# Modulation steps taken in pairs in one layer's merges, moved out of the other's, and put between the seven products; the last down tiles split once

## The chip, the cores and the metric

The kernel runs on one core of a Trainium2 chip. The metric is the device time of one execution in microseconds (us), lower is better. Five engines work side by side, each through its own instructions in a fixed order: TensorE (PE; its weight loads are a row of their own, PEld), VectorE (DVE), ScalarE (ACT), GpSimd (POOL) and SyncE (SP), which here only issues transfers. An instruction whose input or buffer isn't ready holds up everything behind it on its engine.

## The reference

A two-layer generator over 512 latent tokens of width 1024 (with 256 context tokens beside them in layer 0). All is float32.

```python
for l in range(DEPTH):                       # DEPTH = 2
    need_ctx = l < DEPTH - 1
    sh1, sc1, g1, sh2, sc2, g2 = jnp.split(sc @ w_ada[l] + b_ada[l], 6, axis=-1)   # sc = silu(c)
    csh1, ... = jnp.split(scc @ w_ada[l] + b_ada[l], 6, axis=-1)                   # scc = silu(c_ctx)
    h = rmsnorm(x, norm1_g[l]) * (1.0 + sc1) + sh1
    hc = rmsnorm(ctx, norm1_g[l]) * (1.0 + csc1) + csh1
    y, yc = hybrid_mixer(h, hc, w_in[l], ..., need_ctx)
    x = x + g1 * y
    h = rmsnorm(x, norm2_g[l]) * (1.0 + sc2) + sh2
    x = x + g2 * swiglu(h, w_gate, w_up, w_down)
    # with need_ctx the same for ctx
return rmsnorm(x, final_norm_g)

def merge(a, b, c, gate, w_br, w_o):         # the end of hybrid_mixer
    g = jax.nn.sigmoid(gate)                 # gate: the last 3 x 1024 columns of h @ w_in
    m = g[0] * (a @ w_br[0]) + g[1] * (b @ w_br[1]) + g[2] * (c @ w_br[2])
    return m @ w_o
```

`hybrid_mixer` runs windowed attention, a bidirectional gated recurrence and a chunked gating MLP on `h @ w_in`. `w_ada[l]` is 1024 x 6144: six vectors of 1024 (shift, scale and gate for each half of a layer), the "modulation".

## The kernel before, in words

**Dense products.** Activations lie transposed, 128 channels by tokens, and every float32 value is split in two parts (high and low, a rounded float32r and the rest). `dense` multiplies one column tile of 128 weights with all tokens: per 128 rows of the weight three matmuls (high x high, high x low, low x high). Its weights come by `load_w`: one transfer into a raw buffer `wr` (line L283), the high half `wh` written by ACT (L295), the low half `wl` by DVE (L296). The ring of raw buffers has three places, those of `wh` and `wl` two each. `dense` takes weights from the list `early` instead, if something lies there.

**Modulation steps.** The product with `w_ada` isn't done on PE (except for the first four units). A *unit* is 512 of the 6144 columns of one layer, a *step* is 128 of the 1024 rows of one unit: a tile `wra` of 256 KB is loaded, and `ada_accum` adds it, times one scalar per partition, to an accumulator `acc` (the first of a unit's eight steps on ACT, L529, the others on DVE, L531). Layer 0's units and the first four of layer 1 have two accumulators (token and context conditioning), the later ones of layer 1 one. After the eighth step `ada_fold` transposes and sums the accumulator (L506, L507), and after a group of units `ada_spread` sends the sums through eight matmuls or four pairs (L516) into `mod`. The steps wait in a list, `ada_queue`. `fill` does one of them: its tile is loaded one step ahead into the only buffer of the pool `adaw` (L547), so each load is issued after the step before it. `fill_unit` does eight steps by four transfers of 512 KB, two steps each, into the ring `wr` that the weights use too (L629).

**Where they stand.** Layer 0 calls `fill_unit` after the recurrence heads 1 to 3 (24 steps). In the *merges* (three branches of eight column tiles `m`: a gate product `pg`, a branch product `pb`, a tanh on ACT, a multiply on DVE at L1320 or L1323, an add on POOL) `fill` stands twice per tile: in layer 0 in all three branches (48 steps), in layer 1 in the last two (32 steps, units 8 to 11). The feed-forward of layer 0 does 24 + 32 steps: one after each down tile of pieces of four, one after each call of `seven`, the rest in the last down product, which drains the list.

**Feed-forward.** The hidden width is cut in pieces, (4, 2, 4, 4, 4, 4) tiles in layer 0 and (5, 5, 6, 6) in layer 1. From the second piece on, layer 0 makes gate and up by `seven`, a seven-product scheme for two column tiles: three raw loads, four sums on POOL (L435, tiles `s`), four splits by ACT and DVE (L760, L761) and seven products on PE (L413). The last piece's down product runs token block by token block (512 and 256 tokens in layer 0, 256 and 256 in layer 1), so that the next norm can start on the first block while the second is multiplied; each block loads and splits the eight down tiles anew. `add_res` (L808) adds the result to the stream `X`; `start_settle` starts the norm's parts as a chain that is worked off between the products (sums of squares L678 and L680, `nt` L721, high L726 and L730, low L727 on POOL and L731 on DVE). Then `prefetch` loads and splits the first two weight tiles of the next layer.

**What sets the order.** The builder writes the program in one stream; a planner then orders each engine's instructions and transfers by what it expects to be ready, the earlier written first, so a modulation step can run ahead of where it was written. Larger tiles live in 27 `Pages` in on-chip memory, each of two halves, handed out by the builder's own clock.

Of the kernel before, what the change touches and what calls it, by code (L numbers as in the profile page):

```python
# [10 lines left out]
F32R = mybir.dt.float32r  # L11
# [5 lines left out]
P = 128  # L17
D = 1024
KD = 8
# [87 lines left out]
class Builder:  # L107
# [178 lines left out]
    def stationary(self, kt):  # L286
        return [pool.tile([P, KD, P], F32R, tag=tag, name=self.nm(tag))[:, 0:kt, :]
                for pool, tag in ((self.wh, "wh"), (self.wl, "wl"))]

    def load_w(self, wap, kt):  # L290
        nc = self.nc
        raw = self.load_raw(wap, kt)
        hi, lo = self.stationary(kt)
        r, h, o = (t.rearrange("p k c -> p (k c)") for t in (raw, hi, lo))
        nc.scalar.activation(out=h, in_=r, func=AF.Copy)  # L295
        nc.vector.tensor_tensor(out=o, in0=r, in1=h.bitcast(F32), op=ALU.subtract)  # L296
        return hi, lo
# [120 lines left out]
    def seven(self, w1, w2, q, take):  # L418

        nc = self.nc
        n = KD // 2 * P
        r1, r2 = (self.load_raw(w, KD).rearrange("p k c -> p (k c)") for w in (w1, w2))
        r3 = self.load_raw(w2[KD // 2 * P:, :], KD // 2).rearrange("p k c -> p (k c)")
        sa, sb = self.pair("s21"), self.pair("s34")  # L430
        s21, s34 = (t.ap.rearrange("p a b -> p (a b)")[:, 0:2 * n] for t in (sa, sb))
        s2, s1, s3, s4 = s21[:, 0:n], s21[:, n:2 * n], s34[:, 0:n], s34[:, n:2 * n]
        for o, x, y in ((s1, r2[:, 0:n], r2[:, n:2 * n]), (s2, s1, r1[:, 0:n]), (s3, r1[:, 0:n], r2[:, 0:n]),
                        (s4, s2, r1[:, n:2 * n])):
            nc.gpsimd.tensor_tensor(out=o, in0=x, in1=y, op=ALU.add)  # L435
        al = self.pd.tile([P, 1024], F32, tag="pd", name=self.nm("pa"))[:, 0:H]
        be, ga = self.bank("pb")[:, 0:H], self.bank("pg")[:, 0:H]
        tmp = self.single("ptmp")
        u1, u2, u5 = tmp[:, 0:H], tmp[:, H:T], tmp[:, 0:H]
        g1 = self.high_low(r1)  # L440
        self.product(al, g1, 0, q["B11"], True)
        nc.scalar.copy(out=u1, in_=al)
        self.product(be, g1, KD // 2, q["B21"], True)
        take(0, 0, be, u1)
        g2 = self.high_low(s21)
        self.free(sa)
        self.product(al, g2, 0, q["N2"], False)
        nc.scalar.copy(out=u2, in_=al)
        self.product(ga, g2, KD // 2, q["N1"], True)
        nc.scalar.copy(out=u5, in_=ga)  # L450
        g3 = self.high_low(s34)
        self.free(sb)
        self.product(al, g3, 0, q["T3"], False)
        take(1, 1, al, u5)
        self.product(ga, g3, KD // 2, q["B22"], False)
        take(0, 1, ga, u2)
        g4 = self.high_low(r3)
        self.product(al, g4, 0, q["T4"], False)
        take(1, 0, al, None)
        self.free(tmp)  # L460
# [160 lines left out]
            if self.ada_queue:  # L621
                self.ada_load()

    def fill_unit(self):

        assert self.ada_raw is None
        for _ in range(KD // 2):
            raw = self.wr.tile([P, 2, 512], F32, tag="wr", name=self.nm("wra"))
            self.nc.sync.dma_start(out=raw, in_=self.ada_rows_of(2))  # L629
            for j in (0, 1):  # L630
                self.ada_step(raw[:, j, :])
# [623 lines left out]
    def layer(self, l):  # L1255
# [14 lines left out]
        for hd in range(4):  # L1270
            if hd % 2 == 0:
                o.append(self.pair("op"))
            self.hgrn_head(l, hd, act, wcol, o[hd // 2][:, hd % 2, :], need_ctx)
            if hd == 0:
                self.x_out(tt)
            if l == 0 and hd > 0:
                self.fill_unit()
        self.attn_keys(act, wcol)
        at = []
        gm = self.gmlp(l, act, wcol, tt)  # L1280
# [18 lines left out]

        macc = []  # L1300
        if l == 1:
            self.ada_units(1, (8, 9, 10, 11), 1)
        for bi, (idx, src) in enumerate(((2, cc), (0, at), (1, o))):
            if bi == 2:
                self.x_back(tt)
            if bi == 1:
                self.finish_chains()
            br, brheld = self.split_pairs(src, tt, "br")
            for m in range(KD):
                pg = self.dense(wcol(OFF_GT + idx * D + m * P), act, [(0, tt)])  # L1310
                if l == 0 or bi > 0:
                    self.fill()
                gt = self.single("gt")
                nc.scalar.activation(out=gt[:, 0:tt], in_=pg[:, 0:tt], func=AF.Tanh, scale=0.5)
                pb = self.dense(a["w_branch"][l, idx][:, m * P:(m + 1) * P], br, [(0, tt)])
                if bi == 0:
                    if m % 2 == 0:
                        macc.append(self.pair("macc"))
                    mm = macc[m // 2][:, m % 2, 0:tt]
                    nc.vector.scalar_tensor_tensor(out=mm, in0=gt[:, 0:tt], scalar=1.0,  # L1320
                                                   in1=pb[:, 0:tt], op0=ALU.add, op1=ALU.mult)
                else:
                    nc.vector.scalar_tensor_tensor(out=gt[:, 0:tt], in0=gt[:, 0:tt], scalar=1.0,  # L1323
                                                   in1=pb[:, 0:tt], op0=ALU.add, op1=ALU.mult)
                    mm = macc[m // 2][:, m % 2, 0:tt]
                    nc.gpsimd.tensor_tensor(out=mm, in0=mm, in1=gt[:, 0:tt], op=ALU.add)
                self.free(gt)
                if l == 0 or bi > 0:
                    self.fill()
            self.free(*brheld)  # L1330
        self.free(*hheld)
        if l == 0:
            assert len(self.ada_queue) == 3 * KD
            self.ada_units(1, (4, 5, 6, 7), 1)
        else:
            assert not self.ada_queue
        self.dump(f"m{l}", macc[0][:, 0, :])
        mact, mheld = self.split_pairs(macc, tt, "m")
        g1 = self.small("g1", 16).rearrange("p (b k) -> p b k", b=2)
# [21 lines left out]
        for pi, n in enumerate(pieces):  # L1361
            last = pi == len(pieces) - 1
            gu, guheld = [], []
            for i in range(min(n, max(0, plain - f0))):
# [11 lines left out]
                self.split(s[:, 0:tt], hp[:, i % 2, 0:tt], lp[:, i % 2, 0:tt])  # L1376
                self.free(s)
                gu.append((hp[:, i % 2, :], lp[:, i % 2, :]))
                if l == 0 and i > 0:
                    next(making)  # L1380
                    if i > 1:
                        next(making)
# [8 lines left out]
            if last and l == 0:  # L1391
                self.norm_begin(1, ("n1g", 1, 2), 0, 1, "h")
            after = self.norm_shared if l == 0 else self.final_part
            for bi, blk in enumerate(blocks if last else [(None, 0, tt)]):
                for m in range(KD):
                    ps = self.dense(a["w_ffn_down"][l][f0 * P:(f0 + n) * P, m * P:(m + 1) * P], gu, [blk[1:]])
                    for bb in ([blk] if last else blocks):
                        self.add_res(m, ps, lambda b, m: self.mod[l][:, 40 + m, b:b + 1], bb)
                    if n > 2:
                        self.fill()  # L1400
                if last and bi == 0:
                    self.drain()
                self.finish_chains()
                if last and (l == 0 or bi == 0):
                    self.start_settle(blk, after, 0.0 if bi else PACE[1], l == 0)
# [127 lines left out]
```

## Time and profile before

| | |
|---|---|
| Median of 3 runs | 2484.31 us (2484.3 to 2485.63) |
| Profiled execution, its time | 2482.72 us |
| Its span, first to last instruction | 2480.9 us |
| PE busy | 2397.0 us (97%) |
| DVE, ACT, POOL busy | 1555.1, 900.3, 308.9 us |
| Mean granted PE clock | 0.993 |
| Read and written in HBM | 230.45 and 7.34 MB, 96 GB/s over the span |

In the profile, idle time of an engine before an instruction is put down to what released it. The time of a matmul's end is modelled, so a PE that waits a little between matmuls can still be shown as busy; the length of a stretch against the same work in an undisturbed stretch tells more. Tile names are those of the program without their numbers.

### The profile page before, as it was taken

The page shows a single profiled execution, that of the slowest core. Times are in us where ns is not written, and L with a number is a line of the kernel's source. Part 1 is how long each engine was busy: PE and PEld are TensorE (multiplying, and loading weights), DVE is VectorE, ACT ScalarE, POOL GpSimd, SP SyncE. Part 2 cuts the span into 40 slices and gives each one's busy share as a digit, 9 for nine tenths or more (in the row PEclk, how much of TensorE's full clock was granted, in tenths as well). Part 3 has the DMA queues.
Part 4 walks back from the last instruction along what each step waited for, and adds up shares of the span by engine and source line. Part 5 has one row for each costly group of instructions (what it writes and reads, how often), then busy time and mean ns, then how long its engine had stood idle before and what let it go on. Part 6 is the DMA issues. An engine that isn't in the chain of part 4 may idle for free. (4 is left out here: it accounts for less than half of the span.)

```text
span 2480.9 us, 34528 instructions
## 1 busy us (share of the span) xinstructions
PE 2397.0 (97%) x13606; PEld 2083.7 (84%) x13606; DVE 1555.1 (63%) x2644; ACT 900.3 (36%) x1508; POOL 308.9 (12%) x215
## 2 busy tenths in 40 slices
PE   8999999999999999999999989999999999999998
PEld 3888888888788888889999978888887779888888
DVE  4688777875544366767666676678885457434335
ACT  3333344442122243233433453335453235322224
POOL 0000100000111120222232331000000112000001
PEclk9999999999999999999999999999999999999999
DMA  8222111123442241333343341111215455233334
GB/s 295 70 77 81 48 43 35 39 64 112 142 133 73 78 118 43 115 111 110 95 127 111 107 144 52 43 43 52 60 44 152 124 151 168 79 106 100 91 103 130
DMA packets 370673, 240.02 MB, mean 97 GB/s; under 512 B 9744, under 2 KB 341968, under 8 KB 370512
## 3 DMA queue, kind: packets, MB, share of 16 engines
q1 hardware_dynamic: 366576, 225.24, 30.6%
q0 software_dynamic: 2304, 10.49, 1.2%
q8 instruction: 107, 1.75, 0.3%
q10 hardware_dynamic: 1632, 2.10, 0.2%
q14 instruction: 54, 0.44, 0.1%
HBM read 230.45 MB, written 7.34 MB: 96 GB/s over the span
## 5 line engine op out<-in xcount | busy, mean ns | idle before, releaser
L295 ACT ACTIVATE wh<-wr 128x1024 fp32r<-128x1024 f32 (+4 forms) x344 | 308.0, 895 | 853.1 <-PE pd L313 727.2
L313 PE MATMUL pd<-hh,wl 128*128 128x512 f32 (+1 forms) x1504 | 451.9, 356 | 21.5 <-DVE wl L296 21.4
L296 DVE TENSOR_TENSOR wl<-wr,wh 128x1024 fp32r<-128x1024 f32 (+4 forms) x344 | 354.9, 1032 | 186.8 <-ACT wh L295 184.1
L313 PE MATMUL pd<-hh,wh 128*128 128x512 f32 (+1 forms) x1504 | 459.9, 362 | 0.7 <-ACT wh L295 0.6
L313 PE MATMUL pd<-hl,wh 128*128 128x512 f32 (+1 forms) x1504 | 446.7, 354 | 0.0
L313 PEld LDWEIGHTS pd<-hh,wl 128*128 128x128 f32 x1504 | 249.0, 190 | 65.7 <-DVE wl L296 28.9
L531 DVE SCALAR_TENSOR_TENSOR acc<-wra,sc,acc 128x512 f32<-128x512 f32 x224 | 169.6, 778 | 186.7 <-DMA wra<-in_w_ada 175.6
L313 PEld LDWEIGHTS pd<-hl,wh 128*128 128x128 f32 x1504 | 248.2, 190 | 34.4
L313 PEld LDWEIGHTS pd<-hh,wh 128*128 128x128 f32 x1504 | 249.7, 191 | 31.4 <-ACT wh L295 1.0
L313 PE MATMUL pd<-fh,wl 128*128 128x512 f32 (+1 forms) x496 | 175.3, 370 | 0.3 <-DVE wl L296 0.3
L313 PE MATMUL pd<-fl,wh 128*128 128x512 f32 (+1 forms) x496 | 175.7, 370 | 0.0
L313 PE MATMUL pd<-fh,wh 128*128 128x512 f32 (+1 forms) x496 | 174.4, 369 | 0.6 <-ACT silu L1370 0.6
L313 PE MATMUL pd<-guh,wh 128*128 128x512 f32 (+1 forms) x576 | 172.6, 341 | 1.8 <-ACT guh L760 0.9
L313 PE MATMUL pd<-guh,wl 128*128 128x512 f32 (+1 forms) x576 | 172.5, 340 | 1.8 <-DVE wl L296 1.8
L313 PE MATMUL pd<-gul,wh 128*128 128x512 f32 (+1 forms) x576 | 172.9, 340 | 0.1
L808 DVE SCALAR_TENSOR_TENSOR X<-pd,mod,X 128x256 f32<-128x256 f32 (+1 forms) x160 | 84.1, 560 | 85.3 <-PE pd L313 84.9
L313 PEld LDWEIGHTS pd<-guh,wh 128*128 128x128 f32 x576 | 98.3, 188 | 15.4 <-ACT guh L760 1.2
L313 PEld LDWEIGHTS pd<-guh,wl 128*128 128x128 f32 x576 | 98.6, 189 | 15.1 <-DVE wl L296 2.6
L313 PEld LDWEIGHTS pd<-gul,wh 128*128 128x128 f32 x576 | 98.7, 189 | 13.4 <-DVE gul L761 0.9
L313 PEld LDWEIGHTS pd<-fh,wl 128*128 128x128 f32 x496 | 90.1, 188 | 17.4 <-DVE wl L296 1.2
L313 PEld LDWEIGHTS pd<-fh,wh 128*128 128x128 f32 x496 | 89.5, 188 | 16.8 <-ACT silu L1370 0.8
L313 PEld LDWEIGHTS pd<-fl,wh 128*128 128x128 f32 x496 | 90.0, 188 | 15.5
(285 smaller groups left out, 4432.9 us busy)
## 6 DMA issues: line engine op xcount, KB each, us to landing
wr<-in_w_in SPq DMA_DIRECT2D x116, 512.0 KB, 3.9
wra<-in_w_ada SPq DMA_DIRECT2D x136, 256.0 KB, 2.8
wr<-in_w_ffn_gate SPq DMA_DIRECT2D x44, 512.0 KB, 3.9
wr<-in_w_ffn_up SPq DMA_DIRECT2D x44, 512.0 KB, 3.9
wr<-in_w_out SPq DMA_DIRECT2D x32, 512.0 KB, 3.7
wr<-in_w_branch SPq DMA_DIRECT2D x48, 256.0 KB, 3.0
wr<-in_w_ffn_down SPq DMA_DIRECT2D x48, 256.0 KB, 2.8
wr<-in_w_ffn_down SPq DMA_DIRECT2D x24, 384.0 KB, 3.3
```

What stands on the lines that cost most here:

```text
L295: nc.scalar.activation(out=h, in_=r, func=AF.Copy)
L296: nc.vector.tensor_tensor(out=o, in0=r, in1=h.bitcast(F32), op=ALU.subtract)
L313: nc.tensor.matmul(ps[:, b0:b1], lhsT=w[:, k, :], rhs=x[:, b0:b1], start=b not in first, stop=(k == kt - 1 and i == 2), skip_group_check=True)
L531: nc.vector.scalar_tensor_tensor(out=acc[:, 0:512], in0=w, scalar=sc, in1=acc[:, 0:512], op0=ALU.mult, op1=ALU.add)
L808: self.nc.vector.scalar_tensor_tensor(out=self.X[m][:, c0:c1], in0=ps[:, c0:c1], scalar=gcol(b, m), in1=self.X[m][:, c0:c1], op0=ALU.mult, ...
```

## The change

Four edits. (1) In layer 0's merges, one `fill_pairs()` after each column tile (one transfer of 512 KB into `wr`, two steps) takes the place of two `fill` calls. (2) Layer 1's merges do no steps: units 8 and 9 of layer 1 join the list after layer 0's merges and are done in layer 0's feed-forward, units 10 and 11 in layer 1's first gate and up tiles, two pairs after each of the first four. (3) Each `seven` gets one more `fill`, after its second product; layer 1's down products have none. (4) In the last piece of either layer, `keep_w` splits each down tile once, from `wr` into a page, and both token blocks use it through `early`.

```diff
+    def keep_w(self, wap, kt):
+        pg = self.pair("wk", F32R)
+        hi, lo = pg[:, 0, 0:kt * P], pg[:, 1, 0:kt * P]
+        self.split(self.load_raw(wap, kt).rearrange("p k c -> p (k c)"), hi, lo)
+        return pg, tuple(t.rearrange("p (k c) -> p k c", c=P) for t in (hi, lo))
...
         take(0, 0, be, u1)
+        self.fill()
         g2 = self.high_low(s21)
...
-    def fill_unit(self):
-        assert self.ada_raw is None
-        for _ in range(KD // 2):
+    def fill_pairs(self, n=1):
+        for _ in range(n):
+            if not self.ada_queue:
+                return
+            assert self.ada_raw is None
             raw = self.wr.tile([P, 2, 512], F32, tag="wr", name=self.nm("wra"))
             self.nc.sync.dma_start(out=raw, in_=self.ada_rows_of(2))
             for j in (0, 1):
...
             if l == 0 and hd > 0:
-                self.fill_unit()
+                self.fill_pairs(4)
...
         if l == 1:
-            self.ada_units(1, (8, 9, 10, 11), 1)
+            self.ada_units(1, (10, 11), 1)
...
                 pg = self.dense(wcol(OFF_GT + idx * D + m * P), act, [(0, tt)])
-                if l == 0 or bi > 0:
-                    self.fill()
...
                 self.free(gt)
-                if l == 0 or bi > 0:
-                    self.fill()
+                if l == 0:
+                    self.fill_pairs()
...
             self.ada_units(1, (4, 5, 6, 7), 1)
-        else:
-            assert not self.ada_queue
+            self.ada_units(1, (8, 9), 1)
...
                 gu.append((hp[:, i % 2, :], lp[:, i % 2, :]))
-                if l == 0 and i > 0:
+                if l == 1:
+                    self.fill_pairs(2)
+                elif i > 0:
...
-                    ps = self.dense(a["w_ffn_down"][l][f0 * P:(f0 + n) * P, m * P:(m + 1) * P], gu, [blk[1:]])
+                    wap = a["w_ffn_down"][l][f0 * P:(f0 + n) * P, m * P:(m + 1) * P]
+                    if last:
+                        if bi == 0:
+                            kept.append(self.keep_w(wap, n))
+                        self.early.append(kept[m][1])
+                    ps = self.dense(wap, gu, [blk[1:]])
+                    if last and bi == 1:
+                        self.free(kept[m][0])
...
-                    if n > 2:
+                    if l == 0 and n > 2:
                         self.fill()
```

More of the change, by code (lines that the diff above doesn't have):

```diff
@@ L1393, in layer @@
             after = self.norm_shared if l == 0 else self.final_part
+            kept = []
             for bi, blk in enumerate(blocks if last else [(None, 0, tt)]):
                 for m in range(KD):
-                    ps = self.dense(a["w_ffn_down"][l][f0 * P:(f0 + n) * P, m * P:(m + 1) * P], gu, [blk[1:]])
+                    wap = a["w_ffn_down"][l][f0 * P:(f0 + n) * P, m * P:(m + 1) * P]
[6 more added lines that the diff above has]
+                        self.free(kept[m][0])
                     for bb in ([blk] if last else blocks):
                         self.add_res(m, ps, lambda b, m: self.mod[l][:, 40 + m, b:b + 1], bb)
-                    if n > 2:
+                    if l == 0 and n > 2:
                         self.fill()
@@ L1402, in layer @@
                     self.drain()
+                assert l == 0 or not self.ada_queue
                 self.finish_chains()
```

## The prediction

> **What bounds the kernel now.** First the page: which engine fills the span, and what the idle time of the others waits for.
>
> ```profile
> span 2480.9 us, 34528 instructions
> PE 2397.0 (97%) x13606; PEld 2083.7 (84%) x13606; DVE 1555.1 (63%) x2644; ACT 900.3 (36%) x1508; POOL 308.9 (12%) x215
> L531 DVE SCALAR_TENSOR_TENSOR acc<-wra,sc,acc 128x512 f32<-128x512 f32 x224 | 169.6, 778 | 186.7 <-DMA wra<-in_w_ada 175.6
> wra<-in_w_ada SPq DMA_DIRECT2D x136, 256.0 KB, 2.8
> wr<-in_w_in SPq DMA_DIRECT2D x116, 512.0 KB, 3.9
> ```
>
> PE is the bound, and none of the four edits takes a matmul of the model away. All there is to win is time in which PE stands still. The third row says where to look: DVE stood 175.6 us in front of modulation steps whose tile had not landed, with its other work queued behind them. Busy shares don't tell whether PE paid for that, so the second view is the stretches of the changed stages, with undisturbed ones beside them as a rate.
>
> ```profile
> core 0: us, PE busy (x) PEld busy (x) DVE busy (x) ACT busy (x) POOL busy (x), PEclk, DMA share, GB/s
> 552.15:846.89 294.74, 283.95 (x1602) 246.01 (x1601) 146.76 (x207) 70.49 (x92) 34.70 (x19) 0.99 0.37 110
> 754.48:791.92 37.44, 37.44 (x219) 33.01 (x218) 10.52 (x13) 8.03 (x11) 6.70 (x3) 1.00 0.29 85
> 577.85:578.65 0.80, 0.80 (x10) 0.80 (x9) 0.00 (x0) 0.48 (x1) 0.00 (x0) 1.00 0.56 196
> 1878.84:2053.97 175.13, 167.71 (x721) 135.35 (x720) 83.80 (x106) 52.12 (x75) 26.92 (x18) 0.99 0.50 146
> 1953.40:1994.20 40.80, 40.80 (x182) 33.78 (x181) 16.00 (x21) 13.81 (x21) 8.37 (x5) 1.00 0.38 110
> 1024.84:1424.12 399.28, 387.29 (x2195) 366.27 (x2194) 266.24 (x374) 143.01 (x219) 104.33 (x68) 1.00 0.37 108
> 1175.05:1204.17 29.12, 29.12 (x170) 28.94 (x169) 17.89 (x22) 12.48 (x19) 12.68 (x9) 1.00 0.32 92
> 1141.40:1174.68 33.28, 33.21 (x191) 28.81 (x191) 25.14 (x39) 6.97 (x10) 5.33 (x4) 1.00 0.48 144
> 1424.12:1476.85 52.73, 46.19 (x252) 38.86 (x251) 39.97 (x63) 28.46 (x48) 21.58 (x20) 0.97 0.56 164
> 2118.06:2162.02 43.96, 43.92 (x192) 36.07 (x193) 15.12 (x17) 12.38 (x17) 0.00 (x0) 1.00 0.31 90
> 2434.02:2473.50 39.48, 39.48 (x328) 38.84 (x327) 29.53 (x54) 23.06 (x48) 11.47 (x11) 1.00 0.47 143
> ```
>
> Layer 0's merges, 552.15 to 846.89: 1602 matmuls are 22 column tiles of 72 and two spreads of 8 (and two at the edges). Three tiles take 37.44 us undisturbed, 12.48 each, so 22 take 274.56, and the spreads 1.6 (0.80 each). 294.74 - 276.2 = 18.6 us lost. Layer 1's, 1878.84 to 2053.97: 20 tiles of 36 matmuls at 40.80 / 5 = 8.16 us are 163.2, so 11.9 us lost. The stretch of the seven products: 18 calls at 29.12 / 2 = 14.56 (262.1), three down products of four at 33.28 (99.8), one of two at half of that (16.6); 399.28 - 378.5 = 20.7, of which 0.8 is a spread: 19.9 lost. In layer 1's first gate and up tiles and its last down product PE is busy throughout: nothing to win there.
>
> Third, who stopped PE. The first three rows are layer 0's merges, the next two layer 1's, then DVE (658.21, 659.54) and PE at one such place.
>
> ```profile
> DVE acc L531 <- DMA wra<-in_w_ada: 73.1, 34, 6.9
> PEld pd L313 <- DVE wl L296: 13.3, 8, 3.5
> PE pd L313 <- DVE wl L296: 10.8, 8, 3.1
> DVE acc L531 <- DMA wra<-in_w_ada: 57.8, 25, 5.3
> PE pd L313 <- DVE wl L296: 7.3, 6, 3.0
> 658.21 1.42 DVE L531 SCALAR_TENSOR_TENSOR acc<-wra,sc,acc 128x512 f32<-128x512 f32 x2 [3.99 <-DMA wra<-in_w_ada]
> 659.54 1.22 DVE L296 TENSOR_TENSOR wl<-wr,wh 128x1024 fp32r<-128x1024 f32 x1
> 660.81 0.62 PE L313 MATMUL pd<-hh,wl 128*128 128x512 f32 x2 [1.27 <-DVE wl L296]
> ```
>
> DVE waits 3.99 us for a step's tile, then does it, then splits the next gate weight; PE has used up its high half and waits. The tile came late because its load goes out only when the one buffer is free.
>
> **The change part by part.** *Pairs in layer 0's merges.* 48 loads of 256 KB become 24 of 512 KB in the ring of three that the weights use; the steps' DVE and ACT work stays the same. The nearest rows are the heads of layer 0, which already take pairs through that ring (first two rows; heads, 12 pairs), against single loads in the merges (third row):
>
> ```profile
> L629 SPq DMA_DIRECT2D wra<-in_w_ada x12: 367/368/372, 95.5 to 238.2; - x12
> DVE acc L531 <- ACT acc L529: 5.8, 3, 2.2
> L547 SPq DMA_DIRECT2D wra<-in_w_ada x43: 327/328/340, 553.1 to 755.3; - x43
> ```
>
> There DVE waited 5.8 us for 12 pairs, 0.48 each (behind ACT's first step, which waited for the tile); here 73.1 for 43 single loads, 1.7 each. 24 pairs at 0.48 are 11.6 us of waiting, a sixth of 73.1, and a sixth of the 18.6 lost is 3. The ring is busier here than in the heads, so I leave 4.6: **-14**. Ends: -18.6 if all goes; +10 if the weights come late (first rival). On SP the pair stands between the branch load of one tile and the gate load of the next, which therefore waits until the pair before has been accumulated. A serial turn of 3.9 (landing), 4 x 0.78 (accumulations), 3.9 (gate landing) is 10.9 of the 12.48 us that a tile takes: covered, with 1.6 to spare.
>
> *No steps in layer 1's merges.* 32 loads and their accumulations leave; tiles without them run at 8.16 us in the undisturbed stretch. I leave 0.9 of the 11.9: **-11**, ends -11.9 and -8 (waits on POOL's or ACT's part that the steps now hide). The spread at their end moves with the steps.
>
> *16 more steps in layer 0's feed-forward, 18 of its calls to `fill` between products.* Same single buffer, same kind of wait:
>
> ```profile
> DVE acc L531 <- DMA wra<-in_w_ada: 35.6, 32, 2.4
> 1019.50 3.44 DVE L531 SCALAR_TENSOR_TENSOR acc<-wra,sc,acc 128x512 f32<-128x512 f32 x2 [1.20 <-DMA wra<-in_w_ada]
> 1031.74 0.45 PE L413 MATMUL pa<-np,wl 128*128 128x384 f32 x1 [2.07 <-DVE wl L761]
> L761 DVE TENSOR_TENSOR wl<-s,wh x36: 1205/1226/2322, 1030.1 to 1415.1; 128x1024 fp32r<-128x1024 f32 x36
> 1020.65 3.45 POOL L435 TENSOR_TENSOR s<-s,wr 128x512 f32<-128x512 f32 x2
> ```
>
> If every lost microsecond of the stretch were due to its 56 steps, one would cost 19.9 / 56 = 0.36, and 16 more 5.7; at best they fit in DVE's idle third and cost 0. I take **+3**, the middle, since some losses there, as that at 1031.74, come from DVE's backlog and others from POOL's sums, which no step touches. A third group means one more spread on PE: **+0.8**. What stands queued behind an added step: the split of `s` for the next product (1.21 to 2.32 us by its row), then PE; on SP the raw loads of the next call.
>
> The stretched durations in these rows bring in a rule. Two accumulations at 1019.50 took 3.44 us together, where one takes 0.78 on the page, while POOL added: 0.94 more for each. The Trainium skill, "SBUF — State Buffer", section "Who interferes with whom", says that a DVE instruction with two inputs in on-chip memory and a GpSimd instruction that reads it lock each other out, the second waiting for the whole of the first. By it every added step that meets a sum pays for it; the trace agrees in kind. What that would do is the third rival.
>
> *Eight pairs in layer 1's first gate and up tiles.* Four loads of 512 KB in the time of one gate and one up tile, 2 x 43.96 / 8 = 10.99 us, through three places. `w_out`'s loads, the densest there are, are issued thus:
>
> ```profile
> 2085.09 6.91 SPq L283 DMA_DIRECT2D wr<-in_w_out  x3
> ```
>
> Three in 6.91 with the last one's own 0.37, so one per 3.27. Four at that pace take 13.1, 2.1 over, 8.4 for four tiles: the upper end. Lower end 0: PE is never idle here now. Three 3.27 periods fit, so the fourth load slips only if the ring is also late; accumulations (16 x 0.78 = 12.5 us) fit in DVE's idle 28.8. **+2**.
>
> *Last down products split once.* In layer 0's (the stretch from 1424.12) the second block runs while DVE does the first block's norm. First two rows DVE, third ACT, from 1449 on; the last two are PE's waits over the stretch and the longest of them:
>
> ```profile
> L296 DVE TENSOR_TENSOR wl<-wr,wh 128x512 fp32r<-128x512 f32 x6 | 5.5, 913 | 1.1 <-ACT wh L295 1.1
> L296 DVE TENSOR_TENSOR wl<-wr,wh 128x1024 fp32r<-128x1024 f32 x2 | 3.5, 1748 | 0.0
> L295 ACT ACTIVATE wh<-wr 128x512 fp32r<-128x512 f32 x6 | 3.8, 629 | 3.2 <-DMA wr<-in_w_ffn_down 2.5 <-PE pd L313 0.6
> PE pd L313 <- DVE wl L296: 5.1, 4, 3.3
> 1470.89 0.50 PE L313 MATMUL pd<-hh,wl 128*128 128x512 f32 x1 [3.33 <-DVE wl L296]
> ```
>
> Eight splits at 0.913 go from a DVE that is the bound there (23.29 of 26 us busy, by the window row below), and eight loads from the queue ahead of `prefetch`, whose split ends the 3.33 us wait of layer 1's first product. PE waits 5.1 us in all for DVE's splits; the norm's own parts are late next, so I take **-4.5**, ends -5.1 and 0 (the norm takes its pages from what the eight kept ones leave). In layer 1's, PE is busy already: 0; its tail after the last product holds no weight work.
>
> ```profile
> 1449.00:1475.00 26.00, 19.46 (x122) 16.51 (x121) 23.29 (x37) 15.95 (x29) 11.53 (x10) 0.93 0.54 155
> ```
>
> Sum: -14 - 11 + 3 + 0.8 + 2 - 4.5 = -23.7 us. The profiled execution took 2482.7, so 2459.0; the median is 1.6 above it: **2460.6 us**.
>
> **The rivals.** *The pairs starve the weights (slower).* In layer 0's merges a load that takes 5 us instead of 3.9 makes the serial turn 5 + 3.1 + 5 = 13.1, over 12.48, and DVE's split behind it (1.22 in the row above) then lies open. The other edits win 9.7, so with the 18.6 lost now this decides from 28.3 / 24 = 1.2 us per tile on; at 2.0 it is 48 - 28.3 = 19.7 above before: 2504. Against it: the 512 KB loads land in 3.9 at the median. Chance 0.07.
>
> *The wait only changes its tile.* The pair's longer landing makes DVE wait half as often and twice as long, and PE loses what it lost: -2 for -14, so 2472.6. For it: the order on DVE is still fixed ahead, and 34 waits of DVE brought 8 of PE. Against: the heads' 0.48. Chance 0.16.
>
> *Added steps and POOL's sums lengthen each other.* If each of the 16 meets a sum and its 0.94 reaches PE, that is 15 instead of 3: 2472.6. For it: the sums feed the very next product. Against: POOL is busy 104.33 of the stretch's 399.28 us, so one step in four would meet one, and DVE is idle a third of the time. Chance 0.1. *Pages are short.* With eight kept, layer 1's norm waits for them and the 4.5 is not won: 2465.1; chance 0.05.
>
> *All waits go:* -18.6 - 11.9 - 5.1 + 0.8 = -34.8, 2449.5, chance 0.06. Several small ones cancel the gain to within 5 us: 0.06.
>
> **How the numbers follow.** My forecast has 0.5. About 0.2% (5 us) is what a measurement tells from no change. Faster: 0.5 + 0.16 + 0.1 + 0.05 + 0.06 = 0.87, less 0.03 for costs that no row shows, 0.84; same 0.07; slower 0.09, the first rival and a part of that. The range of 2446 to 2480 takes in every case but the first rival and the cancelling one; the likeliest alone spans 2452 to 2469.
>
> **What would show it.** Right: in layer 0's merges DVE's wait for `wra` falls from 73.1 to some 12 us and a tile takes close to 12.48; layer 1's merges run at 8.16 per tile; layer 1's first product waits less than 1 us; PE stays busy through layer 1's gate and up tiles. Wrong: ACT's `wh` waiting for raw weights in the merges; PE's waits for L761 in the seven products growing by more than 6 us; ACT's `wh` waiting for gate or up loads in layer 1.

## The result

The changed kernel takes 2470.39 us (median of 4 runs, 2468.26 to 2472.7), the kernel before 2484.31: a ratio of 0.9948, interval 0.993 to 0.9965, so 13.9 us less. Forecast were 23.7 us less. The sign and the range hold, and 10 us of the forecast gain are missing.

The page after the change: PE's idle time is smaller (77.5 us of the span, 83.9 before), and so is DVE's before the steps (151.7 us in front of L539 where L531 had 186.7). Lines stand 7 to 10 higher than before.

```profile
span 2470.9 us, 34332 instructions
PE 2393.4 (97%) x13614; PEld 2081.4 (84%) x13614; DVE 1535.7 (62%) x2628; ACT 889.6 (36%) x1492; POOL 309.1 (13%) x215
L539 DVE SCALAR_TENSOR_TENSOR acc<-wra,sc,acc 128x512 f32<-128x512 f32 x224 | 169.7, 783 | 151.7 <-DMA wra<-in_w_ada 124.0
```

The same stretches of work as in the prediction, from the view of windows (length, then busy time and count of PE, PEld, DVE, ACT and POOL, granted clock, DMA share, GB/s): layer 0's merges, layer 1's merges, the seven products, layer 0's last down product with layer 1's first products, layer 1's heads up to its merges, its first gate and up work, its second gate and up tiles, its last down product.

```profile
555.88:837.50 281.62, 281.62 (x1602) 244.38 (x1601) 144.02 (x205) 71.04 (x92) 35.09 (x19) 1.00 0.39 116
1875.29:2038.49 163.20, 163.20 (x721) 135.13 (x720) 57.01 (x70) 50.30 (x72) 26.10 (x17) 1.00 0.37 108
1013.97:1429.24 415.27, 392.33 (x2202) 366.90 (x2201) 281.07 (x401) 145.91 (x224) 106.92 (x68) 1.00 0.39 115
1429.24:1473.21 43.97, 43.12 (x249) 37.00 (x249) 28.33 (x47) 21.19 (x36) 20.76 (x19) 1.00 0.42 131
1466.64:1875.29 408.65, 398.80 (x2386) 341.88 (x2385) 305.91 (x612) 177.75 (x347) 35.34 (x25) 1.00 0.18 52
2088.64:2105.78 17.14, 14.34 (x104) 13.75 (x102) 12.67 (x27) 7.10 (x14) 1.15 (x1) 0.90 0.49 145
2105.78:2150.68 44.90, 44.85 (x200) 36.97 (x201) 24.18 (x32) 13.19 (x18) 0.00 (x0) 1.00 0.51 152
2422.68:2463.50 40.82, 39.28 (x328) 38.71 (x326) 18.48 (x42) 13.74 (x35) 8.12 (x11) 1.00 0.08 28
```

PE has no wait left in the merges, which are 13.1 and 11.9 us shorter. Layer 0's last down product and what follows fell from 52.73 to 43.97. The seven products, where the change adds steps, grew from 399.28 to 415.27: **16 us given back in one place**. The last two rows grew by 0.9 (the spread of units 10 and 11) and 1.3, and the row before them by 3.0 (14.1 us before for the same matmuls, at a granted clock of 1.00 where the row has 0.90).

Who stops PE there? First row: layer 0's merges; the others: the seven products.

```profile
DVE acc L539 <- DMA wra<-in_w_ada: 61.4, 16, 5.6
DVE acc L539 <- DMA wra<-in_w_ada: 51.4, 40, 3.2
PE pa L420 <- DVE silu L479: 9.7, 6, 3.1
PEld pa L420 <- DVE silu L479: 11.6, 6, 3.5
```

PE waits for L479, the combine that `take(1, 1)` hands to DVE. The fifth product lies in `pa` until that combine has read it, and the seventh needs `pa`. One such place, from the timeline (SP issues a step's load; DVE waits for it, accumulates, combines; PE goes on):

```profile
1082.30 0.46 SPq L555 DMA_DIRECT2D wra<-in_w_ada  x1
1085.56 1.41 DVE L539 SCALAR_TENSOR_TENSOR acc<-wra,sc,acc 128x512 f32<-128x512 f32 x2 [3.20 <-DMA wra<-in_w_ada]
1086.89 0.55 DVE L479 SCALAR_TENSOR_TENSOR silu<-pa,ptmp 128x384 f32<-128x384 f32 x1
1087.50 0.44 PE L420 MATMUL pa<-fh,wh 128*128 128x384 f32 x1 [2.66 <-DVE silu L479]
```

From this came **theory A**: the added steps cost PE 16 us because combines are queued on DVE behind steps that wait for a tile. Its rivals: the steps' work itself, not the waiting (D); and a step costs PE the same wherever it stands, so that taking it out here loses the same elsewhere.

### The profile page after: what moved, and what is told of

It reads as the page before. It is cut to its first block, busy times and chain, and to the rows that moved or that the text cites. A ratio compares the mean times of both kernels' runs of the same rounds, so it can differ in the third digit from the quotient of the medians.

```text
span 2470.9 us, 34332 instructions
## 1 busy us (share of the span) xinstructions
PE 2393.4 (97%) x13614; PEld 2081.4 (84%) x13614; DVE 1535.7 (62%) x2628; ACT 889.6 (36%) x1492; POOL 309.1 (13%) x215
## 5 line engine op out<-in xcount | busy, mean ns | idle before, releaser
L302 ACT ACTIVATE wh<-wr 128x1024 fp32r<-128x1024 f32 (+4 forms) x312 | 284.5, 912 | 802.2 <-PE pd L320 688.6
L303 DVE TENSOR_TENSOR wl<-wr,wh 128x1024 fp32r<-128x1024 f32 (+4 forms) x312 | 324.5, 1040 | 209.2 <-ACT wh L302 206.8
L539 DVE SCALAR_TENSOR_TENSOR acc<-wra,sc,acc 128x512 f32<-128x512 f32 x224 | 169.7, 783 | 151.7 <-DMA wra<-in_w_ada 124.0
L320 PE MATMUL pd<-guh,wh 128*128 128x512 f32 (+1 forms) x416 | 123.9, 354 | 1.4 <-ACT guh L770 0.9
L320 PE MATMUL pd<-gul,wh 128*128 128x512 f32 (+1 forms) x416 | 124.7, 356 | 0.4 <-DVE gul L771 0.2
L320 PE MATMUL pd<-guh,wl 128*128 128x512 f32 (+1 forms) x416 | 123.4, 353 | 0.0
L320 PEld LDWEIGHTS pd<-fh,wh 128*128 128x128 f32 x496 | 90.6, 190 | 17.1 <-ACT silu L1377 1.3
L690 POOL TENSOR_TENSOR sqa<-sqa,sq 128x256 f32<-128x256 f32 (+1 forms) x40 | 48.2, 1206 | 418.9 <-ACT sq L688 400.3
L1334 POOL TENSOR_TENSOR macc<-macc,gt 128x768 f32<-128x768 f32 (+1 forms) x32 | 62.2, 1943 | 269.0 <-DVE gt L1331 269.0
L320 PE MATMUL pd<-brl,wh 128*128 128x512 f32 (+1 forms) x288 | 87.7, 359 | 0.0
```

The costliest lines, as they stand in the source:

```text
L320: nc.tensor.matmul(ps[:, b0:b1], lhsT=w[:, k, :], rhs=x[:, b0:b1], start=b not in first, stop=(k == kt - 1 and i == 2), skip_group_check=True)
L539: nc.vector.scalar_tensor_tensor(out=acc[:, 0:512], in0=w, scalar=sc, in1=acc[:, 0:512], op0=ALU.mult, op1=ALU.add)
L690: eng.tensor_tensor(out=acc[:, c0:c1], in0=acc[:, c0:c1], in1=sq[:, c0:c1], op=ALU.add)
```

## The experiments

All kernels are edits of the changed one; of an edit the main lines are shown, `...` marks what is left out. Stretches run from the same matmul to the same matmul, so that they can be set side by side.

**No step between the products (e1_nomid).** Its 16 steps go to layer 0's merges, as a second pair per tile in the last branch.

```diff
         take(0, 0, be, u1)
-        self.fill()
...
-                    self.fill_pairs()
+                    self.fill_pairs(2 if bi == 2 else 1)
...
```

> The changed kernel without the step between the seven products; eight more pairs in the last branch of layer 0's merges do those 16 steps, so the feed-forward does 56 steps where it did them before. The stretch from the first to the last call of the seven products was 399.3 us before and 415.3 after. Theory A (the added steps make DVE wait for their tile, with the combining of two products, and so PE, queued behind): the stretch returns to 400 +- 3, and the merges stay at 12.5 to 12.8 us per tile with two pairs in each of eight tiles: about 2456 us. Rival B (the stretch is longer for another reason: kept pages, a slower rhythm of PE, the spreads): it stays at 411 or more, 2468 or more. Rival C (two pairs in one tile are too many for the ring of raw buffers): the stretch returns, but the last branch of the merges loses 8 us or more.

Measured: 2465.33 us (2462.24 to 2466.49), ratio 0.9922 [0.9905, 0.9939]. Layer 0's merges, `w_out` (the product that ends the mixer), the seven products:

```profile
555.23:843.34 288.11, 283.01 (x1603) 244.19 (x1602) 165.95 (x238) 73.05 (x96) 35.10 (x19) 1.00 0.44 127
843.34:921.31 77.97, 72.19 (x398) 62.57 (x397) 46.00 (x56) 31.44 (x42) 20.27 (x12) 0.96 0.37 107
1024.79:1422.50 397.71, 389.49 (x2203) 368.43 (x2202) 252.94 (x362) 143.87 (x220) 105.56 (x69) 0.99 0.37 110
```

The seven products are back at 397.7, so the added step alone makes the 16 us. But the merges (281.62 in the changed kernel) and `w_out` (73, at a clock of 1.00 where this row has 0.96) are 11.5 us longer: 2456 us as by theory A is missed, the merges lose 6.5 where rival C had 8 or more, and that place was no good.

**Tiles two ahead (e2_two).** The single loads go into halves of pages, two ahead.

```diff
-        self.ada_raw = self.aw.tile([P, 1, 512], F32, tag="aw", name=self.nm("wra"))
+        pg = self.single("wra")
+        raw = pg[:, 0:512].rearrange("p (k c) -> p k c", k=1)
...
-            if self.ada_queue:
+            while len(self.ada_raws) < min(2, len(self.ada_queue)):
                 self.ada_load()
...
```

> The changed kernel with the single loads of the modulation steps kept two ahead, in halves of pages, instead of one ahead in one buffer; the number of steps and their places are those of the changed kernel. Theory A (what costs is the wait for the tile, because the load goes out only after the step before): DVE's wait for these tiles in the stretch of the seven products falls from 51 us to 15 or less and the stretch from 415 to 400 or less, about 2456 us or less. Rival D (what costs is the work of the steps on DVE, and its contention with POOL's sums): the wait falls, but the stretch stays at 410 or more and the time within 4 us of 2470.

Measured: 2463.44 us (2461.04 to 2466.98), ratio 0.9917 [0.9899, 0.9936]. First the waits in the seven products, then the stretch in the view of windows:

```profile
PE pa L420 <- DVE silu L479: 12.6, 6, 2.9
DVE acc L539 <- DMA wra<-in_w_ada: 10.2, 8, 2.9
```

```profile
1010.88:1418.57 407.69, 389.87 (x2203) 368.62 (x2201) 279.86 (x390) 144.64 (x222) 101.04 (x68) 0.99 0.38 115
```

DVE's wait fell from 51.4 to 10.2, the stretch by 7.6 only, between what theory A (400 or less) and rival D (410 or more) expected, and PE stands before the combine as long as ever. Theory A alone is at best half of it.

**The last down tiles split twice again (e3_resplit).**

```diff
-                        if bi == 0:
-                            kept.append(self.keep_w(wap, n))
-                        self.early.append(kept[m][1])
...
```

> The changed kernel with the last down tiles loaded and split anew for each block, as before. If the splits taken from the second block are what shortened layer 0's last down product and the start of layer 1 (52.7 us before, 45.5 after): it returns to 51 to 54, and the wait of 1.5 us at the start of layer 1's last down product, which came with the kept tiles, goes: together 4 to 7 us slower than the changed kernel, 2474 to 2477. Rival (that stretch is shorter because no step is left in it, or because PE arrives later): it stays at 47 or less, and the time at 2470 or less.

Measured: 2475.02 us (2469.56 to 2477.32), ratio 0.9959 [0.9945, 0.9972]. The stretch of layer 0's last down product and what follows, and layer 1's last down product:

```profile
1421.67:1471.82 50.15, 45.66 (x251) 38.11 (x251) 37.29 (x60) 27.78 (x48) 21.53 (x20) 0.97 0.57 167
2420.68:2460.16 39.48, 39.48 (x328) 38.85 (x327) 29.52 (x54) 23.05 (x48) 11.47 (x11) 1.00 0.47 143
```

50.15 against 43.97: the edit is worth 6.2 us there, of which some 1.5 go with the lower granted clock of the row (0.97; the changed kernel has 1.00). In layer 1 it costs 1.3 (39.48 against 40.82): its splits run ahead on ACT and DVE, and the last tile of the hidden layer is split behind them. The one wait of PE in that stretch of the changed kernel:

```profile
PE pd L320 <- ACT guh L770: 1.5, 1, 1.5
```

**Layer 1's pairs in its merges (e4_l1merge).** Units 10 and 11 as one pair per tile of the second branch, none in the gate and up tiles.

```diff
-                if l == 0:
+                if l == 0 or bi == 1:
                     self.fill_pairs()
...
-                if l == 1:
-                    self.fill_pairs(2)
...
```

> The changed kernel with layer 1's eight pairs (units 10 and 11) one per tile in the second branch of layer 1's merges instead of in its first gate and up tiles. If the pairs run ahead into the norm of the second block and take DVE from it: the stretch from the end of layer 1's merges to its second gate tile, 67.3 us after and 64.1 before, returns to 64 or less, the merges stay at 8.16 us per tile (20 tiles 163.2), and the time falls by 3 to 5 us, 2466. Rival (a ring of three can't feed gate, branch and pair in 8.16 us): the eight tiles lose 1 us or more each, and the time stays or rises.

Measured: 2475.07 us (2474.31 to 2476.3), ratio 0.9962 [0.9949, 0.9975]. Layer 1's merges, its first gate and up work:

```profile
1872.07:2044.13 172.06, 167.56 (x730) 136.70 (x728) 71.42 (x90) 51.30 (x74) 25.39 (x17) 0.99 0.42 127
2093.49:2107.64 14.15, 12.96 (x104) 12.24 (x102) 9.36 (x22) 6.48 (x13) 0.71 (x1) 1.00 0.29 84
```

The first gate work falls from 17.14 to 14.15 and the second tile from 44.90 to 44.0, so the pairs cost 3.9 us where the change put them. In the merges they cost 8.9, 1.1 per tile (each figure holds their spread of 0.8): pairs are not free as such, and the rival's 1 us per tile came true. Layer 1's tile takes 8.16 us and holds less than layer 0's 12.5.

**No tile loaded, nothing to wait for (e5_noload).**

```diff
             self.ada_step(self.ada_raw[:, 0, :])
-            self.ada_raw = None
-            if self.ada_queue:
-                self.ada_load()
...
```

> Left out: all single loads of modulation tiles but the first; each such step adds the same loaded tile again, so the modulation of layer 1 is another. All accumulations stay where they are, and nothing waits for a tile. Theory A (the stretch of the seven products lost its 16 us to combines queued on DVE behind steps that wait for tiles): DVE's waits for modulation tiles vanish and the stretch falls from 415.3 to 400 us or less, near the 399.3 of the kernel before. Theory D (the steps' work on DVE itself, stretched where POOL adds, holds the combines up): the stretch stays at 406 or more, and PE goes on waiting for the first combine of the second half. Between the two both have a share.

**The same, with the step between the products in layer 1's heads (e10_noload_nomid).** The edit that takes the step out is that of e7_heads1 below.

> The single loads but the first are left out as in e5_noload (the modulation of layer 1 is another), and the step between the seven products is taken out, its 16 steps standing after layer 1's heads. With e5_noload (408.4 us for the stretch of the seven products) it gives the price of the 16 added steps where no step waits for a tile. If the waits of the steps that were there before cost PE something too, the stretch falls below e7_heads1's 399.9, to 390 or less; if only the added steps stand in PE's way, it stays at 396 to 401, and their price without waits is some 8 to 9 us.

**Both again, with POOL's sums replaced by copies on ACT (e11_noload_copies, e12_noload_nomid_copies).**

```diff
-            nc.gpsimd.tensor_tensor(out=o, in0=x, in1=y, op=ALU.add)
+            nc.scalar.copy(out=o, in_=x)
...
```

> As e5_noload, and the four sums of each call of the seven products, which POOL makes, are replaced by copies of their first operand on ACT (the products, and so the result, are others; the amount of work on PE and DVE is the same). Theory P (what the added steps cost beside waiting comes from POOL's sums: both last longer when they meet): accumulations take 0.75 to 0.80 us again instead of 1.0, and the difference of this run's stretch to that of e12_noload_nomid_copies is 3 us or less, where e5_noload and e10_noload_nomid differ by some 8. Rival Q (it comes from the place, on DVE's queue ahead of a combine for which PE waits): accumulations get shorter, but the difference stays at 6 us or more.

> As e11_noload_copies without the step between the seven products: its 16 steps stand after layer 1's heads. The stretch of this kernel is the base for e11_noload_copies: P expects the two within 3 us, Q this one at least 6 us shorter. Against e10_noload_nomid (sums on POOL, no step in the middle) it shows what POOL's sums cost the stretch by themselves: if the next product's split waits for the last sum, 3 us or more.

One profile of each (2467.59, 2450.95, 2443.39, 2436.74 us). The seven products in e5, e10, e11, e12, in this order:

```profile
1015.90:1424.27 408.37, 393.25 (x2200) 372.96 (x2201) 275.15 (x383) 144.57 (x222) 109.68 (x68) 0.98 0.26 77
```

```profile
1010.16:1403.56 393.40, 387.30 (x2192) 368.37 (x2193) 254.99 (x360) 143.58 (x219) 104.53 (x68) 0.99 0.27 79
```

```profile
1011.13:1401.09 389.96, 385.21 (x2203) 365.63 (x2201) 245.84 (x380) 181.28 (x290) 0.00 (x0) 1.00 0.28 80
```

```profile
1007.58:1392.34 384.76, 383.29 (x2195) 365.19 (x2194) 234.50 (x357) 180.44 (x288) 0.00 (x0) 1.00 0.28 81
```

| seven products, us | step between the products | step elsewhere | price of the 16 steps |
|---|---|---|---|
| tiles loaded, sums on POOL (changed kernel, e7) | 415.3 | 399.9 | 15.4 |
| no loads, sums on POOL (e5, e10) | 408.4 | 393.4 | 15.0 |
| no loads, no sums on POOL (e11, e12) | 390.0 | 384.8 | 5.2 |

**Theory A as the whole cause falls.** With nothing to wait for, e5's stretch is 408.4 where A wanted 400 or less, and the 16 steps still cost 15.0; e10's 393.4 lies between its two cases, and its 8 to 9 us as the price without waits is missed. Each price holds the third group's spread, 0.8. Two things in these rows keep the table from giving shares.

The first is the granted clock (the figure after POOL's in each row): PE had half of it for 17.1 us of e5's stretch, for 6.8 of e10's, for 3.4 of the changed kernel's and of e7's, and not at all in e11's and e12's. Two of e5's pieces:

```profile
1072.04:1075.45 3.41, 3.41 (x11) 3.41 (x12) 3.41 (x7) 2.37 (x4) 0.70 (x1) 0.50 0.51 147
1293.91:1300.73 6.82, 5.97 (x19) 5.97 (x20) 6.12 (x10) 2.00 (x3) 0.00 (x0) 0.50 0.44 129
```

At most half of these times was lost by it: 8.5, 3.4, 1.7 and 1.7 us. Without them the three prices are 15.4, some 10 and 5.2. With one profile each, the price without waits lies between 10 and 15, and the waiting's share between nothing and a third.

The second is that the steps, freed of their wait, met something else. DVE's accumulations in the stretch of the changed kernel, then of e5 and of e11, and the splits of sums in the last two:

```profile
L539 DVE SCALAR_TENSOR_TENSOR acc<-wra,sc,acc 128x512 f32<-128x512 f32 x72 | 57.6, 808 | 51.6 <-DMA wra<-in_w_ada 51.4
```

```profile
L539 DVE SCALAR_TENSOR_TENSOR acc<-wra,sc,acc 128x512 f32<-128x512 f32 x58 | 56.8, 992 | 2.1 <-ACT acc L537 1.6
L767 DVE TENSOR_TENSOR wl<-s,wh 128x1024 fp32r<-128x1024 f32 x36 | 51.7, 1436 | 8.6 <-ACT wh L766 8.1
```

```profile
L539 DVE SCALAR_TENSOR_TENSOR acc<-wra,sc,acc 128x512 f32<-128x512 f32 x56 | 41.1, 747 | 5.2 <-ACT acc L537 4.7
L767 DVE TENSOR_TENSOR wl<-s,wh 128x1024 fp32r<-128x1024 f32 x36 | 44.0, 1221 | 12.7 <-ACT wh L766 12.4
```

In e5 20 of the 58 accumulations overlap one of POOL's sums, and these take 1.46 us on average, the others 0.75 as in e11: 14.2 us of DVE in all. In the changed kernel only 6 of 72 overlap one, in e7 3 of 58; with tiles two ahead (e2) it is 19 of 69. So e5 isn't the changed kernel with the wait alone taken out: its accumulations don't stay where they were, as was expected of it, but fall onto the sums. What the Trainium skill, "SBUF — State Buffer", section "Who interferes with whom", states, that a DVE instruction with two inputs in on-chip memory contends with GpSimd's reads and one with a single such input doesn't (two-port modes aside), agrees: the combine L479, which has one input there, takes 556 ns in both.

What all these rows have in common is the combine queued on DVE behind the steps. PE's matmuls wait for L479 14.0 us in the changed kernel (9.7 and 4.3 by its two rows), 4.6 in e7 (where it is L478), 12.6 in e2 and 10.9 in e5:

```profile
PE pa L420 <- DVE ptmp L479: 6.1, 3, 3.2
PE pa L420 <- DVE silu L479: 4.8, 2, 2.7
```

In e11, with neither waits nor sums, no wait of a matmul for it is left, and the price is 5.2, between the 3 of P and the 6 of Q. By these rows late tiles held the combine up in the changed kernel and lengthened steps in e5: where one goes the other takes over. Their shares aren't shown. The copies on ACT are also shorter (0.62 us, against 1.5 to 1.7 for a sum), so a split's input is ready earlier; how much of the step from 15 (or 10) to 5.2 is the lengthening and how much that, stays open.

**Where the steps land.** The added steps shift the whole list. The four calls of the second piece made by `seven`, before and after, and DVE's accumulations in them:

```profile
1079.04:1141.39 62.35, 60.81 (x338) 59.60 (x337) 36.17 (x46) 26.31 (x40) 22.94 (x16) 0.97 0.29 83
```

```profile
L531 DVE SCALAR_TENSOR_TENSOR acc<-wra,sc,acc 128x512 f32<-128x512 f32 x2 | 1.4, 749 | 0.0
```

```profile
1068.90:1141.52 72.62, 62.63 (x338) 59.45 (x337) 50.74 (x64) 26.34 (x42) 24.40 (x16) 0.98 0.35 106
```

```profile
L539 DVE SCALAR_TENSOR_TENSOR acc<-wra,sc,acc 128x512 f32<-128x512 f32 x16 | 14.0, 885 | 14.8 <-DMA wra<-in_w_ada 14.8
```

Before, the planner had two accumulations on DVE there and twelve in the down product behind them, where POOL adds nothing. With a step in each call it is sixteen, because these steps still have two accumulators each, and 10.3 of the 16 us are lost in these four calls. Their number alone doesn't do it: with 21 accumulations, no waits and no sums these calls take 60.95 us in e11.

**Pairs instead of single steps (e9_pairs7).** One pair after each call, one after every second down tile, none between the products.

```diff
                 self.seven(col(name, i), col(name, i + 1), q, take)
-                self.fill()
+                self.fill_pairs()
...
```

> The same 72 steps in layer 0's feed-forward as in the changed kernel, but as pairs of 512 KB: one pair after each call of the seven products instead of one single step in the middle and one after it, and one pair after every second down tile. Theory A (the tile that comes late does the harm): DVE's waits for tiles in the stretch fall from 51 us to under 20 and the stretch from 415.3 to 402 or less. Rival (a pair in the ring of weights holds up the raw loads of the next call, and its two to three microseconds of accumulations in a row hold up a combine as long as a wait does): the stretch stays at 411 or more.

Measured: 2480.45 us (2475.25 to 2484.05), ratio 0.9986 [0.9976, 0.9997]. The rival holds: the stretch is the longest of all, and PE waits for splits that DVE makes late (the stretch, and PE's longest waits in it).

```profile
1010.97:1434.00 423.03, 393.56 (x2202) 372.22 (x2201) 262.68 (x390) 146.27 (x224) 102.68 (x72) 0.98 0.39 114
```

```profile
PE pa L420 <- DVE wl L770: 24.2, 13, 3.3
```

**The 16 steps in layer 1's heads (e7_heads1).**

```diff
         take(0, 0, be, u1)
-        self.fill()
...
+            if l == 1 and hd > 0:
+                if hd == 1:
+                    self.ada_units(1, (8, 9), 1)
+                self.fill_pairs((3, 3, 2)[hd - 1])
...
```

> The step between the seven products is taken out; its 16 steps (units 8 and 9 of layer 1) are done in pairs after the recurrence heads 1 to 3 of layer 1 (3, 3 and 2 pairs). Theory A and D alike say that the stretch of the seven products returns to 397 to 400 us with nothing lost in the merges (281.6 and 163.2 stay). Theory H (DVE, about 72% busy in layer 1's heads, takes 16 x 0.78 us there beside PE): that stage, 408.7 us, grows by at most 3, and the time is about 2458 where the changed kernel has 2471, a ratio of 0.990 to the kernel before. Rival (a step costs PE the same wherever it stands, some 0.9 us): the heads of layer 1 grow by 10 us or more and the time stays within 4 us of the changed kernel.

Measured: 2455.8 us (2454.54 to 2457.12), ratio 0.9892 [0.9877, 0.9906], no overlap with the changed kernel's interval. The seven products; layer 1's heads up to its merges:

```profile
1010.84:1410.74 399.90, 387.30 (x2195) 366.67 (x2193) 267.76 (x378) 145.28 (x222) 104.48 (x68) 1.00 0.37 110
1448.20:1858.57 410.37, 399.74 (x2394) 343.05 (x2393) 313.21 (x632) 178.61 (x349) 35.15 (x25) 1.00 0.21 61
```

The same 16 steps that cost 15.4 there cost 1.7 here (410.37 against 408.65): the rival falls, the place decides. By the profiled executions another 3.7 us of the gain aren't the edit's: layer 0's merges took 277.9 here, at PE's faster pace (last section).

**All late steps in the heads, none between the products or in layer 1's gate and up tiles, pages for down tiles in layer 0 alone (e8_allheads).**

```diff
+            if l == 1 and hd > 0:
+                if hd == 1:
+                    self.ada_units(1, (8, 9, 10, 11), 1)
+                self.fill_pairs((5, 5, 6)[hd - 1])
...
-                    if last:
+                    if last and l == 0:
...
```

> All of layer 1's units 8 to 11 are done in pairs after the recurrence heads 1 to 3 of layer 1 (5, 5 and 6 pairs), none between the seven products and none in layer 1's gate and up tiles, and the down tiles of the last piece are kept in pages in layer 0 alone. Worked out from the runs so far: e7_heads1's 2455.8, less 3.9 (first gate tile and second tile of layer 1, as the run with pairs in layer 1's merge showed), less 1.4 (last down product of layer 1, as the run with two splits showed), plus 1.7 for 16 more steps in the heads (what e7_heads1 paid for its 16): 2452, ratio 0.9875. Rival: 32 steps in three heads are too many for DVE and for the ring of raw buffers (5 or 6 pairs in a row stand ahead of a head's weights), layer 1's heads grow by 8 us or more over the changed kernel's 408.7, and the time is above 2457.

Measured: 2451.39 us (2447.97 to 2452.06), ratio 0.9864 [0.9846, 0.9881], against 2452 worked out. Layer 1's heads and its first gate and up work:

```profile
1444.65:1859.10 414.45, 401.72 (x2395) 344.39 (x2394) 323.75 (x652) 179.98 (x351) 35.09 (x24) 1.00 0.24 70
2071.94:2086.09 14.15, 12.96 (x105) 12.25 (x103) 9.36 (x22) 6.50 (x13) 0.71 (x1) 1.00 0.29 83
```

The second 16 steps cost the heads 4.1 us, not 1.7, and won 3.9 in the gate and up tiles: no gain from that half. The rest comes from layer 1's last down product (1.3 by e3) and from differences between executions. It beats both kernels; e7_heads1's interval overlaps with it.

## Why the prediction was right or wrong

- **Pairs in layer 0's merges, -14: 13.1, right by luck.** The step that gave it was wrong: DVE's wait for `wra` was to fall to 12 us, a sixth, and fell from 73.1 to 61.4. But PE has no wait left in the stretch, which is more than forecast. So the premise of the second rival (half as many waits, twice as long) came true and its price did not: with one wait per tile instead of two, DVE still made the next split in time. That the split's place behind the wait decides is argued from the rows, not tried by itself. The 5.4 us over 276.2 are PE's slower pace (last section), which took back what the waits gave beyond the forecast; the prediction knew nothing of it.
- **No steps in layer 1's merges, -11: right.** 20 tiles at 8.16 to the digit, no leftover.
- **16 more steps in the feed-forward, +3 and +0.8: the step that failed.** It measured 16.0 with the spread, and 15.4 against the same steps in layer 1's heads, far beyond the upper end of 5.7 and 0.8. That end was an average, the loss of the stretch before divided by its 56 steps. What a step costs depends on where it lands: in the four calls that lost most, the kernel before had two accumulations on DVE and the changed one sixteen, ahead of combines that free `pa` for PE. That path, from step to combine to PE, stands nowhere in the prediction, which looked at the split of `s`: PE's waits for that split grew from 5.1 to 5.6 us only, those for the combine from 4.2 to 14.0. The third rival (added steps and POOL's sums lengthen each other, 15 instead of 3) had the size by luck: in the changed kernel 6 of 72 accumulations meet a sum, fewer than its one in four. Its mechanism is real (1.46 us against 0.75) and takes over where the waits are gone, in e5 and e2.
- **Pairs in layer 1's gate and up tiles, +2:** 3.9 by e4, with their spread, within its ends; part of it is the granted clock of 0.90 in the first gate work, which the prediction hadn't counted.
- **Last down tiles split once, -4.5 and 0:** 6.2 by e3 in layer 0, beyond the end of 5.1: I had counted PE's waits for DVE's splits alone, and nothing for the lower clock of the stretch that has them (0.97), some 1.5. All in all it fell by 8.8; 2.6 of that belong to no edit that was tried. In layer 1 it costs 1.3, where I had put 0 because PE was busy: a busy PE can only lose.
- **Against the profiled executions:** spans 2480.9 and 2470.9. -13.1 (layer 0's merges) - 11.9 (layer 1's) + 16.0 - 8.8 (last down product with layer 1's first products) + 4.1 (layer 1's `w_out`, gate and up) + 1.3 (its last down product) make -12.4; the first products of the run, 2.97 longer in the profiled execution after, and 0.7 less in layer 0's heads and `w_out`, make -10.1, to 0.1 the difference of the spans.

## What to carry to other kernels

The price of a filler step is not its duration nor an average over its kind: read from the windows where the planner really puts the fillers, and ask what stands behind them on their engine and who waits for it. Before putting the cost of a delayed engine down to the wait that the profile names, take that wait away, and then look at what took its place: here the freed steps met POOL's sums and cost PE 10 to 15 us still. A 2 x 2 of short runs (step in or out, suspected cause in or out) shows that by differences alone, if the granted clock of the four is the same; set it beside the times first.

## What was not expected of the hardware

**PE has two steady paces for the same stream.** Six matmuls of 512 and 256 tokens in turn take 1.040 or 1.060 us, so a tile of layer 0's merges 12.48 or 12.72, with no wait and the clock at 1.00. Every undisturbed group of six in the changed kernel's merges ran at the slow one (22 x 0.24 = 5.3 us, the 5.4 left over); in e3_resplit, the same program up to there, some 190 ran at the fast one, and the stretch took 277.79. In these two and in the kernel before, which has both paces, it changes only where something comes between, a spread or a wait. To test that, e6_break puts one dummy matmul before each tile:

```diff
+                if l == 0:
+                    bk = self.bank("dm")
+                    nc.tensor.matmul(bk[:, 0:P], lhsT=br[0][0][:, 0:P], rhs=br[0][0][:, 0:P], start=True, stop=True)
```

> One more matmul of 128x128 on data already there, its result unused, before each of the 24 column tiles of layer 0's merges; nothing else changes. Theory R (PE has two steady rhythms for groups of 512 and 256 tokens, 1.040 and 1.060 us for six matmuls, and passes from one to the other only where its stream is interrupted): the 24 interruptions make both rhythms appear, with changes only at them, and the stretch of 22 tiles ends between 277 and 283 us. Rival (the rhythm is fixed by the program or by what the other engines do in the stretch): every group stays at 1.060 as in the changed kernel, and the stretch is 281.6 plus 22 times the added matmul, 283 or more.

Measured: 2473.45 us, one run; the stretch of the 22 tiles, with its spreads and dummies, took 281.4 us, within theory R's 277 to 283. Three neighbouring tiles:

```profile
604.52:617.12 12.60, 12.60 (x75) 11.04 (x74) 8.52 (x12) 2.38 (x4) 0.00 (x0) 1.00 0.29 91
617.12:629.95 12.83, 12.83 (x76) 11.16 (x75) 5.31 (x7) 3.85 (x6) 0.00 (x0) 1.00 0.25 71
629.95:642.55 12.60, 12.60 (x76) 11.03 (x74) 5.43 (x7) 2.38 (x4) 0.64 (x1) 1.00 0.57 181
```

The pace turns at every single dummy, fast, slow, fast, through all 22 tiles. What in PE holds it is open. It moves the merges by some 4 us (281.62 and 277.79) between kernels that are the same up to there; whether it does so between runs of one kernel, no second profile shows.

**A short wait can cost twice.** The first products of the run took 14.85 us before and 17.82 after, with a program that is the same up to there; of the fourteen profiles, four had the long form. There PE had waited 1.6 us for DVE, and the granted clock was lower (0.90):

```profile
47.50:62.35 14.85, 14.67 (x78) 12.16 (x77) 10.42 (x23) 6.46 (x13) 0.00 (x0) 1.00 0.37 94
```

```profile
47.45:65.27 17.82, 16.21 (x78) 13.32 (x78) 12.22 (x25) 6.65 (x14) 0.00 (x0) 0.90 0.30 81
```

The Trainium skill, "TensorE: Matmul & The Clock Gate", section "What's actually happening", puts the drop to half the clock at an idle window of about 3.4 us; here the clock fell behind a wait of 1.6 to 1.8 us, in all four profiles that have it and in none of the ten others. The length alone doesn't decide: in the changed kernel the nine microseconds behind PE's waits of 1.96 us (ending at 1020.76) and 3.13 (at 1032.17) ran at 1.00. In layer 1's first gate and up work (17.14 us at 0.90, 14.15 at 1.00 in e4) the pairs' price is in part a lower clock too; what brought it on there wasn't tried.
